# A diffusion transformer layer: half of the conditioning sum computed on ScalarE and GpSimd instead of VectorE

## The chip, the cores and the metric

The kernel runs on one core of one Trainium2 chip. The metric is the device time of one execution in microseconds (us), as the median of several runs. TensorE does the matmuls (PE in the profile, PEld its weight loads), VectorE is DVE, ScalarE is ACT, GpSimd is POOL, and SyncE (SP) issues nearly all transfers.

## The reference, cut to what matters

One layer with 1024 latent tokens and 256 context tokens, 1024 features, all in fp32. It is half a SwiGLU feed-forward, then token mixing (a 2-D Fourier transform beside a bidirectional chunkwise mLSTM), then the second half of the feed-forward. Each part is normalised and modulated by a shift, a scale and a gate that come from a conditioning vector:

```python
def ada_params(cvec, w, b):
    m = jax.nn.silu(cvec) @ w + b
    return m.reshape(cvec.shape[0], N_ADA, 1, D_MODEL)

def half_ffn(h, shift, scale, gate, g_pre, g_post, w13, w2):
    u = modulate(rmsnorm(h, g_pre), shift, scale)
    return h + 0.5 * gate * rmsnorm(swiglu(u, w13, w2), g_post)
...
    ml = ada_params(c, w_ada[l], b_ada[l])
    mc = ada_params(c_ctx[None], w_ada[l], b_ada[l])
    h_lat = half_ffn(h_lat, ml[:, 0], ml[:, 1], ml[:, 2], g[0], g[1], w13_a[l], w2_a[l])
    h_ctx = half_ffn(h_ctx, mc[:, 0], mc[:, 1], mc[:, 2], g[0], g[1], w13_a[l], w2_a[l])
```

There are two conditioning vectors, one for the latent tokens and one for the context, and both meet the same matrix `w_ada` (1024 x 9216), which is read in nine chunks of 1024 columns. Of these the context stream needs the first five.

## The kernel before

**The products.** Feed-forward products on the latent tokens use Winograd's scheme for 2 x 2 blocks: seven products in place of eight. Every fp32 operand is split in two parts, `hi` (cast on ScalarE, L145) and `lo` (the rest, subtracted on VectorE, L146), and `mm3` (L153) makes three matmuls of them. So each operand tile costs one ScalarE cast and one VectorE subtraction before TensorE can use it.

**The stage around the change.** `wino_out` is the second product of the feed-forward half. Its seven products (in the order 1, 6, 7, 4, 5, 3, 2) each run over 11 blocks of features and 4 column blocks of 128. For each block it loads weights (`raw` into `wr`, L733, or `held` into `g`, L738), combines them on VectorE (L727), splits them into `wh` and `wl`, loads the activations (`t<-gx`, L774) and splits these into `g` tiles. "The first second product" is the call in the first half of the layer.

**The background work.** Beside the matmuls, `tick` (called once per three matmuls) takes steps of generators that `later` has put in a list. During the first second product these are: the context tokens being loaded and transposed (`load_x`), the conditioning sums of chunks 2 and 3 (`ada_rest`, L239), the normalised context (`prenorm`), the conditioning sums of chunk 4, and, as results come, the residual sums.

**The conditioning sum.** For each half chunk (512 columns) `ada_rest` loads eight tiles of `w_ada` of 128 x 512 (L247) and sums them, weighted per partition by the conditioning vector, into one accumulator for each stream: a plain scaling for the first tile (L251) and `acc = t * sc + acc` for the other seven (L253), on VectorE. The two accumulators are then split, summed over the partitions by four matmuls with a selecting matrix (L263), copied (L266), turned into a column (L275) and given their bias (L279). Stream 0 is the latent, stream 1 the context. Tiles come from the pool `u` (16 buffers of 128 x 512) in chunks 2 and 3; in chunk 4 the weight tiles come from `wa` (two buffers).

**What sets the order.** The kernel is written for a scheduler that takes each instruction's place in the program as its priority, puts the instructions of each engine in a fixed order, gives tiles their buffers and adds the semaphores. Every engine then runs its own list strictly in order, and so does SP's queue of transfers. A change of who computes what can therefore move other instructions too.

Of the kernel before, what the change touches and what calls it, by code (L numbers as in the profile page):

```python
# [12 lines left out]
AF = mybir.ActivationFunctionType  # L13
ALU = mybir.AluOpType
# [5 lines left out]
CTX = 256  # L20
# [14 lines left out]
class Kernel:  # L35
# [200 lines left out]
            nc.scalar.copy(row[:2, :], pt[:2, :])  # L236
            self.ada_cols(row, (0, 1), ch, 0)

    def ada_rest(self, streams, chunks, tags=("wa", "u", "u", "b"), halves=(0, 1)):  # L239
        nc = self.nc  # L240
        w = self.a["w_ada"][0]
        for ch in chunks:
            for hf in halves:
                acc = {s: self.s512(tags[1]) for s in streams}
                for k in range(ND):
                    t = self.s512(tags[0])
                    nc.sync.dma_start(t, w[k * P : (k + 1) * P, ch * D + hf * TB : ch * D + (hf + 1) * TB])  # L247
                    yield
                    for s in streams:
                        if k == 0:  # L250
                            nc.vector.tensor_scalar_mul(acc[s], t, self.sc[:, k, s : s + 1])  # L251
                        else:
                            nc.vector.scalar_tensor_tensor(acc[s], t, self.sc[:, k, s : s + 1], acc[s],  # L253
                                                           op0=ALU.mult, op1=ALU.add)
                yield
                for s in streams:
                    ah, al = self.s512(tags[2], F32R), self.s512(tags[2], F32R)
                    self.split_act(ah, al, acc[s])
                    if s == streams[0]:
                        pr = self.aux()  # L260
                    yield
                    for i, part in enumerate((ah, al)):
                        nc.tensor.matmul(pr[:2, :], self.sel[:, s, :], part, start=s == streams[0] and i == 0,  # L263
                                         stop=s == streams[-1] and i == 1)
                row = self.s512(tags[3])
                nc.scalar.copy(row[:2, :], pr[:2, :])  # L266
                yield
                self.ada_cols(row, streams, ch, hf)
# [1333 lines left out]
    def run(self):  # L1602
        nc, a = self.nc, self.a
# [6 lines left out]
        xl, xc = [[], []], []  # L1610
# [3 lines left out]
        u = self.new_u()  # L1614
# [17 lines left out]
        for p in range(3):  # L1632
# [5 lines left out]
        gx = self.scratch([7, FF // 2, TB], "gx")  # L1638
        rc1, r1 = [], [[], []]
        self.ffn_in(w13, 11, u, U, gx, 6, mid)  # L1640
        self.later(self.load_x(a["ctx"][0], CTX, "c", xc, tag="u"), self.ada_rest([0, 1], [2, 3], "uuuu"),
                   rate=3.5)
        self.credit = -9.0
        uc = ctx_u([self.slot("u", F32R) for _ in range(ND)])

        def ctx_in():
            yield from self.prenorm(self.reload(xc[0], CTX), xc[1:], CTX, 1, 0, uc)
            yield from self.ada_rest([0, 1], [4])
        self.later(ctx_in(), rate=3.5)
        res = [[None] * ND for _ in range(NB)]  # L1650

# [32 lines left out]
        for b in range(NB):  # L1684
# [3 lines left out]
            t = self.s512("o")  # L1688
# [16 lines left out]
        for h in range(HEADS):  # L1705
# [11 lines left out]
            k = [self.qk_proj(8 + 2 * h + i, u2) for i in range(2)]  # L1717
# [19 lines left out]
        for b in range(NB):  # L1737
# [8 lines left out]
            if b == 0:  # L1746
                u = self.new_u()
# [62 lines left out]
```

## Time and profile before

| | |
|---|---|
| median of 3 runs | 2758.67 us (2755.25 to 2763.62) |
| the profiled execution's own time | 2761.97 us |
| its span in the profile | 2760.1 us |
| busy: PE, DVE, ACT, POOL | 2661.3, 1857.2, 1106.8, 100.6 us |
| the first second product | from 490.0 us to 744.1 us |

The span is what the profiler saw between the first and the last instruction; what lies around it is 1.9 us. TensorE's busy time hides small gaps, because matmuls overlap and their ends are modelled, so the number of matmuls in a stretch says more than its busy time. In a row of groups the columns are: line, engine, operation, output and inputs, shapes, count, then total busy time and mean duration in ns, and the engine's idle time before those instructions with what ended it. In a row of the timeline the first number is the start and the second the length of a run of equal instructions.

### The profile page before, as it was taken

The page shows a single profiled execution, that of the slowest core. Times are in us where ns is not written, and L with a number is a line of the kernel's source. Part 1 is how long each engine was busy: PE and PEld are TensorE (multiplying, and loading weights), DVE is VectorE, ACT ScalarE, POOL GpSimd, SP SyncE. Part 2 cuts the span into 40 slices and gives each one's busy share as a digit, 9 for nine tenths or more (in the row PEclk, how much of TensorE's full clock was granted, in tenths as well). Part 3 has the DMA queues.
Part 4 walks back from the last instruction along what each step waited for, and adds up shares of the span by engine and source line. Part 5 has one row for each costly group of instructions (what it writes and reads, how often), then busy time and mean ns, then how long its engine had stood idle before and what let it go on. Part 6 is the DMA issues. An engine that isn't in the chain of part 4 may idle for free.

```text
span 2760.1 us, 33923 instructions
## 1 busy us (share of the span) xinstructions
PE 2661.3 (96%) x11657; PEld 2114.7 (77%) x11657; DVE 1857.2 (67%) x3341; ACT 1106.8 (40%) x1893; POOL 100.6 (4%) x217
## 2 busy tenths in 40 slices
PE   8899999998999999999999999999999999998998
PEld 5688888776877777777777778778887788887776
DVE  5688887899786438565363674555667887863765
ACT  4543332444454337233333333433345433333552
POOL 1100000000000001000000000000001000000000
PEclk9999999999999999999999999999999999999999
DMA  9765454857686545325223452356556654536874
GB/s 300 242 206 164 155 167 133 309 190 252 210 252 211 170 134 173 102 69 155 79 77 103 133 142 77 94 150 196 181 157 210 183 169 153 168 107 198 293 247 139
DMA packets 426012, 472.51 MB, mean 171 GB/s; under 512 B 25497, under 2 KB 264642, under 8 KB 425840
## 3 DMA queue, kind: packets, MB, share of 16 engines
q1 hardware_dynamic: 424448, 468.53, 54.2%
q0 software_dynamic: 1248, 1.75, 0.2%
q8 instruction: 92, 1.51, 0.2%
q14 instruction: 80, 0.66, 0.1%
q10 hardware_dynamic: 144, 0.07, 0.0%
HBM read 373.21 MB, written 97.04 MB: 170 GB/s over the span
## 4 chain that ended last, share of the span: by engine, by line
PE 75%; DVE 9%; DMA 8%; issue 4%; ACT 2%; SPq 1%; POOL 0%; DVEq 0%; POOLq 0%; ACTq 0%
PE mm L153 67%; DMA m<-r_l 2%; PE aux L1147 2%; PE qc L1332 1%; DVE u L253 1%; DVE wl L141 1%; DVE g L146 1%; DMA ld<-in_w_ada_dram 1%; DMA ld<-h 1%; DMA u<-h 1%; DMA ld<-hn 1%; PE mm L234 1%; DMA t<-gx 0%; ACT wh L140 0%; DVE wl L146 0%
## 5 line engine op out<-in xcount | busy, mean ns | idle before, releaser
L153 PE MATMUL mm<-g,wh 128*128 128x512 f32 (+1 forms) x2552 | 839.6, 409 | 11.9 <-ACT g L145 5.0
L153 PEld LDWEIGHTS mm<-g,wh 128*128 128x128 f32 (+1 forms) x2552 | 484.2, 192 | 122.2 <-ACT wh L145 6.0
L153 PE MATMUL mm<-g,wl 128*128 128x512 f32 (+1 forms) x1276 | 510.7, 402 | 3.4 <-DVE wl L146 3.3
L153 PE MATMUL mm<-g,o 128*128 128x512 f32 x2112 | 497.7, 394 | 0.0
L153 PEld LDWEIGHTS mm<-g,o 128*128 128x128 f32 x2112 | 396.9, 188 | 93.7
L141 DVE TENSOR_TENSOR wl<-wr,wh 128x1024 fp32r<-128x1024 f32 x226 | 278.8, 1234 | 223.9 <-ACT wh L140 223.2
L140 ACT CAST wh<-wr 128x1024 fp32r<-128x1024 f32 x226 | 236.3, 1046 | 352.5 <-PE mm L153 307.3
L153 PE MATMUL mm<-wh,g 128*128 128x512 f32 x1032 | 331.2, 399 | 6.6 <-ACT g L145 3.9
L153 PEld LDWEIGHTS mm<-g,wl 128*128 128x128 f32 (+1 forms) x1276 | 243.8, 191 | 59.0 <-DVE wl L146 5.6
L153 PE MATMUL mm<-u,wh 128*128 128x512 f32 (+1 forms) x848 | 268.4, 398 | 7.5 <-DVE m L704 4.9
L153 PEld LDWEIGHTS mm<-wh,g 128*128 128x128 f32 x1032 | 194.1, 188 | 54.5 <-ACT g L145 4.1
L153 PE MATMUL mm<-wl,g 128*128 128x512 f32 x516 | 205.1, 397 | 0.0
L153 PEld LDWEIGHTS mm<-u,wh 128*128 128x128 f32 (+1 forms) x848 | 159.8, 190 | 46.0 <-DVE m L704 5.4
L153 PE MATMUL mm<-wh,u 128*128 128x512 f32 x544 | 176.4, 399 | 0.0
L153 PE MATMUL mm<-u,wl 128*128 128x512 f32 (+1 forms) x424 | 167.3, 397 | 2.3 <-DVE wl L141 2.3
L582 DVE TENSOR_TENSOR t<-mm,t 128x512 f32<-128x512 f32 x128 | 88.1, 688 | 78.8 <-PE mm L153 78.6
L146 DVE TENSOR_TENSOR g<-t,g 128x512 fp32r<-128x512 f32 x154 | 103.0, 687 | 38.9 <-ACT g L145 32.1
L153 PEld LDWEIGHTS mm<-wh,u 128*128 128x128 f32 x544 | 102.0, 188 | 22.5
L145 ACT CAST o<-wa 128x512 fp32r<-128x512 f32 x88 | 54.6, 622 | 156.0 <-PE mm L153 144.8
L145 ACT CAST wh<-wr 128x1024 fp32r<-128x1024 f32 (+1 forms) x72 | 62.5, 870 | 131.9 <-PE mm L153 55.2
L153 PEld LDWEIGHTS mm<-wl,g 128*128 128x128 f32 x516 | 97.2, 188 | 23.0 <-issue 0.7
L153 PE MATMUL mm<-wl,u 128*128 128x512 f32 x272 | 108.8, 400 | 2.1 <-DVE wl L141 2.1
(469 smaller groups left out, 3432.8 us busy)
## 6 DMA issues: line engine op xcount, KB each, us to landing
wr<-in_w_a_dram SPq DMA_DIRECT2D x124, 512.0 KB, 4.4
t<-gx SPq DMA_DIRECT2D x174, 256.0 KB, 4.0
wr<-in_w_in_dram SPq DMA_DIRECT2D x80, 512.0 KB, 3.8
wr<-in_w_b_dram SPq DMA_DIRECT2D x70, 512.0 KB, 4.5
gx<-m SPq DMA_DIRECT2D x88, 256.0 KB, 4.2
gx<-t SPq DMA_DIRECT2D x66, 256.0 KB, 4.3
ld<-in_w_ada_dram SPq DMA_DIRECT2D x64, 256.0 KB, 2.8
ld<-h SPq DMA_DIRECT2D x48, 256.0 KB, 3.8
```

Source lines behind the costliest of these rows:

```text
L140: nc.scalar.copy(hv, rv)
L141: nc.vector.tensor_tensor(lv, rv, hv.bitcast(F32), op=ALU.subtract)
L145: self.nc.scalar.copy(hi, src)
L146: self.nc.vector.tensor_tensor(lo, src, hi.bitcast(F32), op=ALU.subtract)
L153: mul = lambda x, y, start, stop: self.nc.tensor.matmul(out, x, y, start=start, stop=stop, skip_group_check=grown)
L234: nc.tensor.matmul(pt[:2, :], self.sc[:, k, :], t, start=k == 0, stop=k == ND - 1)
L253: nc.vector.scalar_tensor_tensor(acc[s], t, self.sc[:, k, s : s + 1], acc[s], op0=ALU.mult, op1=ALU.add)
L582: add = lambda o, x, y: nc.vector.tensor_tensor(o, x, y, op=ALU.add)
L1147: nc.tensor.matmul(pt[:, :257], kw[:, i * P : (i + 1) * P], vaug, start=True, stop=True)
L1332: nc.tensor.matmul(pt[:, :257], at(q, i, c), C[:, i * 257 : (i + 1) * 257], start=i == 0, stop=i == 1)
```

## The change

`ada_rest` gets a switch `shared`, on in the two calls beside the first second product (chunks 2, 3 and 4, thus six halves). With it, the context stream's term is computed in two steps: ScalarE multiplies the tile by the conditioning vector (the first one straight into the accumulator, the others into a new tile of the pool `u`), and GpSimd adds the new tile to the accumulator. The latent stream stays on VectorE. The two other calls of `ada_rest` stay as they were.

```diff
-    def ada_rest(self, streams, chunks, tags=("wa", "u", "u", "b"), halves=(0, 1)):
+    def ada_rest(self, streams, chunks, tags=("wa", "u", "u", "b"), halves=(0, 1), shared=False):
...
                     for s in streams:
-                        if k == 0:
+                        if shared and s == 1:
+                            part = self.s512(tags[1]) if k else acc[s]
+                            nc.scalar.activation(part, t, AF.Copy, scale=self.sc[:, k, s : s + 1])
+                            if k:
+                                nc.gpsimd.tensor_tensor(acc[s], acc[s], part, op=ALU.add)
+                        elif k == 0:
                             nc.vector.tensor_scalar_mul(acc[s], t, self.sc[:, k, s : s + 1])
...
-        self.later(self.load_x(a["ctx"][0], CTX, "c", xc, tag="u"), self.ada_rest([0, 1], [2, 3], "uuuu"),
+        self.later(self.load_x(a["ctx"][0], CTX, "c", xc, tag="u"), self.ada_rest([0, 1], [2, 3], "uuuu", shared=True),
...
-            yield from self.ada_rest([0, 1], [4])
+            yield from self.ada_rest([0, 1], [4], shared=True)
```

The lines of the changed kernel stand six further down from the accumulating step on: L253 becomes L259, L727 becomes L733, L774 becomes L780; the load of the weight tile is L248 there, the new scaling on ScalarE L253 and the new addition L255.

The scheduler gives the whole stage another order. On VectorE, in a half of chunk 3 of the kernel before (`u_5154` and `u_5155` are the two accumulators, `u_5187` and so on the weight tiles):

```order
721 L146 TENSOR_TENSOR g_5273<-t_5270,g_5272 128x512
722 L727 TENSOR_TENSOR wr_5317<-wr_5317,g_4260 128x512
723 L253 SCALAR_TENSOR_TENSOR u_5154<-u_5187,sc,u_5154 128x512
724 L253 SCALAR_TENSOR_TENSOR u_5155<-u_5187,sc,u_5155 128x512
725 L253 SCALAR_TENSOR_TENSOR u_5154<-u_5197,sc,u_5154 128x512
726 L253 SCALAR_TENSOR_TENSOR u_5155<-u_5197,sc,u_5155 128x512
727 L253 SCALAR_TENSOR_TENSOR u_5154<-u_5207,sc,u_5154 128x512
728 L253 SCALAR_TENSOR_TENSOR u_5155<-u_5207,sc,u_5155 128x512
```

The same engine in a half of chunk 3 in the changed kernel (`u_4991` is the latent accumulator):

```order
694 L259 SCALAR_TENSOR_TENSOR u_4991<-u_5015,sc,u_4991 128x512
695 L146 TENSOR_TENSOR g_5520<-t_5517,g_5519 128x512
696 L146 TENSOR_TENSOR g_5526<-t_5523,g_5525 128x512
697 L146 TENSOR_TENSOR g_5582<-t_5579,g_5581 128x512
698 L146 TENSOR_TENSOR g_5588<-t_5585,g_5587 128x512
699 L259 SCALAR_TENSOR_TENSOR u_4991<-u_5048,sc,u_4991 128x512
700 L146 TENSOR_TENSOR wl_5307<-wr_5308,wh_5306 128x1024
701 L146 TENSOR_TENSOR g_5649<-t_5646,g_5648 128x512
702 L146 TENSOR_TENSOR g_5700<-t_5697,g_5699 128x512
703 L146 TENSOR_TENSOR g_5706<-t_5703,g_5705 128x512
704 L259 SCALAR_TENSOR_TENSOR u_4991<-u_5060,sc,u_4991 128x512
```

The context steps are gone, and the latent ones no longer stand next to each other: three to four instructions of the product lie between two of them.

On ScalarE in the changed kernel, at the end of that half (`u_4992` is the context accumulator, `u_5126` the last of the scaled tiles that GpSimd adds to it):

```order
439 L253 ACTIVATE u_5114<-u_5105,sc 128x512
440 L145 CAST g_5831<-t_5829 128x512
441 L145 CAST g_5837<-t_5835 128x512
442 L253 ACTIVATE u_5126<-u_5117,sc 128x512
443 L145 CAST wh_5509<-wr_5511 128x1024
444 L145 CAST u_5135<-u_4991 128x512
445 L145 CAST g_5892<-t_5890 128x512
446 L145 CAST u_5169<-u_4992 128x512
447 L145 CAST g_5898<-t_5896 128x512
```

The scalings stand between the casts of the product's operands, and the cast of the finished context accumulator stands four places behind the last scaling.

In SP's queue of transfers, the kernel before and then the changed one, in a half of chunk 3 (`u` are weight tiles of the conditioning, `t` and `wr` tiles of the product):

```order
419 L774 DMA t_5467<-gx 128x512
420 L247 DMA u_5187<-in_w_ada_dram 128x512
421 L247 DMA u_5197<-in_w_ada_dram 128x512
422 L247 DMA u_5207<-in_w_ada_dram 128x512
423 L247 DMA u_5217<-in_w_ada_dram 128x512
424 L247 DMA u_5240<-in_w_ada_dram 128x512
425 L247 DMA u_5278<-in_w_ada_dram 128x512
426 L247 DMA u_5288<-in_w_ada_dram 128x512
```

```order
415 L248 DMA u_5015<-in_w_ada_dram 128x512
416 L780 DMA t_5646<-gx 128x512
417 L780 DMA t_5697<-gx 128x512
418 L780 DMA t_5703<-gx 128x512
419 L248 DMA u_5048<-in_w_ada_dram 128x512
420 L780 DMA t_5758<-gx 128x512
421 L780 DMA t_5764<-gx 128x512
422 L780 DMA t_5829<-gx 128x512
423 L248 DMA u_5060<-in_w_ada_dram 128x512
```

Seven loads in a row became one load behind every three others. The matmuls of the product itself keep their order; the last matmuls of the conditioning sum (L263) stand behind matmul 658 of the stage's 924 before, and behind matmul 790 in the changed kernel.

## The prediction

> **What bounds the kernel now.** I read the page's head, then the stretch the change touches: the second product of the first feed-forward half, whose background loop holds the edited generator. Its first and last matmuls, two in mid-stage, and busy time in pieces (columns: length, busy time and instructions of PE, PEld, DVE, ACT, POOL, granted clock, DMA share, GB/s):
>
> ```profile
> span 2760.1 us, 33923 instructions
> 490.00 1.52 PE L153 MATMUL mm<-g,wh 128*128 128x512 f32 x2 [4.96 <-ACT g L145]
> 519.27 0.62 PE L153 MATMUL mm<-g,wh 128*128 128x512 f32 x2
> 519.95 0.62 PE L153 MATMUL mm<-g,wh 128*128 128x512 f32 x2
> 744.12 0.39 PE L153 MATMUL mm<-wh,u 128*128 128x512 f32 x1
> 490.00:540.00 50.00, 50.00 (x206) 39.88 (x207) 42.47 (x71) 24.40 (x43) 0.00 (x0) 0.94 0.86 309
> 540.00:590.00 50.00, 44.48 (x180) 33.22 (x179) 46.51 (x79) 20.90 (x39) 0.00 (x0) 0.93 0.59 200
> 590.00:640.00 50.00, 46.35 (x202) 36.15 (x202) 46.90 (x79) 24.66 (x42) 0.00 (x0) 1.00 0.74 237
> 640.00:690.00 50.00, 44.46 (x169) 32.19 (x168) 44.99 (x68) 23.60 (x36) 0.00 (x0) 0.90 0.77 247
> 690.00:744.00 54.00, 53.90 (x248) 44.41 (x247) 41.27 (x64) 23.87 (x37) 2.40 (x2) 1.00 0.69 219
> ```
>
> The stage runs from 490.0 to 744.1: 254.1 us. It holds 924 matmuls (7 products x 11 x 4 x 3). Three take 519.95 - 519.27 = 0.68, so 0.229 each and 211.6 for all; the 24 that sum the conditioning and the small transposes add some 10. So 33 us are lost, about 5 of them at the start (the matmuls stand 0.43 apart until 496, at a lower clock). The other 28 lie between 540 and 690, where DVE is busy 138 of 150 us, ACT 69 and POOL never. DVE is what PE waits for there, directly or through ACT:
>
> ```profile
> ACT wh L145 <- DVE g L727: 19.5, 9, 6.4
> ACT wh L145 <- DVE wr L727: 16.1, 4, 6.8
> ACT u L145 <- DVE u L253: 12.6, 5, 4.4
> L253 DVE SCALAR_TENSOR_TENSOR u<-u,sc,u 128x512 f32<-128x512 f32 x56 | 37.9, 745 | 0.3 <-DMA u<-in_w_ada_dram 0.3
> L253 DVE SCALAR_TENSOR_TENSOR u<-wa,sc,u 128x512 f32<-128x512 f32 x28 | 19.5, 748 | 4.1 <-DMA wa<-in_w_ada_dram 4.1
> 590.29 0.88 DVE L251 TENSOR_SCALAR u<-u,sc 128x512 f32<-128x512 f32 x2 [1.01 <-DMA u<-in_w_ada_dram]
> 594.42 9.37 DVE L253 SCALAR_TENSOR_TENSOR u<-u,sc,u 128x512 f32<-128x512 f32 x14 [0.31 <-DMA u<-in_w_ada_dram]
> 603.71 1.22 DVE L146 TENSOR_TENSOR wl<-wr,wh 128x1024 fp32r<-128x1024 f32 x1
> 604.84 0.68 DVE L146 TENSOR_TENSOR u<-u,u 128x512 fp32r<-128x512 f32 x1
> 605.45 0.68 DVE L146 TENSOR_TENSOR g<-t,g 128x512 fp32r<-128x512 f32 x1
> ```
>
> 84 accumulating steps of the conditioning stand in this stage, in bursts of up to 14. DVE's instructions overlap, so I cost them by their pitch: 14 take 9.37, hence (9.37 - 0.74)/13 = 0.66 per step; 0.40 per plain scaling (0.88 - 0.48); 1.13 for 128x1024 (604.84 - 603.71); 0.60 for 128x512 (605.45 - 604.84).
>
> A check by these pitches: up to the matmul numbered 673 of the stage, DVE must have done (counted in the program's order, up to the write that matmul waits for) 148 of 0.60, 84 of 0.66, 12 of 0.40, 16 of 1.13, 16 half-size ones of 0.40 and small ones for 1: 175.4 us. PE's 672 matmuls take 153.9. DVE is 21.5 behind at its worst point, which is most of the 28.
>
> **The change, part by part.** *Removed from DVE:* 42 steps and 6 scalings: 42 x 0.66 + 6 x 0.40 = 30.1 us. The bursts go too: in the new order one step stands every four or five DVE instructions. The same count for the new order is worst at two places. Before matmul 577 DVE has 147 of 0.60, 28 of 0.66, 4 of 0.40, 13 of 1.13: 124.2 against PE's 131.9, 7.7 ahead. Before matmul 721 it has 166, 35, 5, 20 and 16 half-size: 155.1 against 164.9, 9.8 ahead. If nothing else happened, DVE would no longer hold PE up.
>
> *Added on GpSimd:* 42 additions of 128x512 from SBUF. The trace has 16 such, and DVE beside them:
>
> ```profile
> L455 POOL TENSOR_TENSOR b<-u,u 128x512 f32<-128x512 f32 x8 | 17.5, 2192 | 150.0 <-ACT b L367 79.4 <-DVE g L146 47.4 <-DVE acc L341 23.2
> L456 POOL TENSOR_TENSOR wa<-u,u 128x512 f32<-128x512 f32 x8 | 12.0, 1502 | 35.2 <-DVE u L409 13.0 <-ACT m L678 11.2 <-DVE g L146 6.6
> 128.73 1.65 POOL L456 TENSOR_TENSOR wa<-u,u 128x512 f32<-128x512 f32 x1 [1.23 <-DVE m L475]
> 131.00 1.70 POOL L455 TENSOR_TENSOR b<-u,u 128x512 f32<-128x512 f32 x1 [0.63 <-DVE g L146]
> 135.74 1.28 POOL L456 TENSOR_TENSOR wa<-u,u 128x512 f32<-128x512 f32 x1 [3.03 <-DVE g L146]
> 129.17 1.75 DVE L146 TENSOR_TENSOR g<-b,g 128x512 fp32r<-128x512 f32 x1
> 130.85 0.74 DVE L458 SCALAR_TENSOR_TENSOR ld<-ld,pre,rb 128x512 f32<-128x512 f32 x1
> 131.51 1.75 DVE L146 TENSOR_TENSOR g<-b,g 128x512 fp32r<-128x512 f32 x1
> 2133.50 2.97 POOL L455 TENSOR_TENSOR b<-u,u 128x512 f32<-128x512 f32 x1 [7.89 <-DVE g L146]
> 2135.22 0.68 DVE L704 TENSOR_TENSOR m<-mm,t 128x512 f32<-128x512 f32 x1
> 2135.82 1.20 DVE L146 TENSOR_TENSOR g<-wa,g 128x512 fp32r<-128x512 f32 x1
> ```
>
> A DVE instruction with two inputs in SBUF, 0.68 alone, takes 1.75 when it starts under a GpSimd addition: 1.07 more, until the addition is nearly over. The one that reads PSUM (mm) at 2135.22 keeps its 0.68, and the next loses only 0.52. Where DVE was idle nothing is lost. Over the 16 additions DVE's instructions are longer by 9.1 us, 0.57 each, with 0 and 1.07 as the ends. In this stage DVE reads PSUM in only some two dozen instructions, but without the 30 us it has more gaps. I take s = 0.75 per addition, between the mean and the end, for the stage is denser than the mean.
>
> The Trainium skill's page "SBUF — State Buffer", section "Who interferes with whom", says that DVE and GpSimd share a port pair, that a DVE instruction with two SBUF inputs contends with a GpSimd instruction that reads SBUF, and that the later one waits for the whole of the earlier. Taken to the letter an addition costs its own length, 1.28, and the change loses; the rows bear out the wait, but for 1.07 at most and less beside PSUM reads.
>
> With s, DVE's lag is 28s - 7.7 at matmul 577 and 35s - 9.8 at 721: for s = 0.57, 8.3 and 10.2; for 0.75, 13.3 and 16.5; for 1.05, 21.7 and 27.0. Against 21.5 before, s = 0.75 gains 5.0. The trace lost 28 where this count gives 21.5 (each wait is followed by matmuls at a lower clock, 0.90 to 0.93 above), so I scale by 1.3: **-6.5 us**, between -17 (s = 0.5, lag 7.7) and +7 (s = 1.05).
>
> *Added on ACT:* 48 scalings.
>
> ```profile
> 745.46 1.15 ACT L340 ACTIVATE b<-o 128x512 f32<-128x512 f32 x2
> L145 ACT CAST u<-u 128x512 fp32r<-128x512 f32 x12 | 7.3, 620 | 12.7 <-DVE u L253 12.6
> u<-in_w_ada_dram SPq DMA_DIRECT2D x32, 256.0 KB, 5.3
> ```
>
> Two take 1.15, so 0.52 each, 25 us in all. ACT is busy 117 of the stage's 254 us, so its length is hidden; without that cover it would cost the 25. What counts is order: the cast of the finished sum (u<-u) stands in ACT's queue, with the casts of PE's operands behind it, and now waits for the last addition on GpSimd instead of DVE's last step. The old wait was 12.6 over five casts. The last addition follows the last scaling by its own 1.3 to 1.7, and a late chain adds one more addition: some 2 to 3 us in each of six halves. Bounds -5 to +10; I take **+2**.
>
> *Moved: the weight loads.* SP's queue issued seven of a half's eight loads in a row; now one stands behind every two to four others, and both DVE and ACT use it six or so DVE instructions after the release that lets SP reach it. Six instructions are 4 us plus one s, the landing 5.3 (median). So up to 1 us of wait per load, on two in-order engines, where a half used to pay it once. Part falls into time in which GpSimd adds anyway. 32 loads: 0 to +15; I take **+2**. The 14 loads into two wa buffers waited before (4.1 above) and still do.
>
> *Behind the stage:* eight fewer DVE instructions of other work are done at its last matmul, so 8 x 0.60 = 5 us of DVE work pass into the next stage: 0 to +3, taken **+1**.
>
> Sum: -6.5 + 2 + 2 + 1 = -1.5. The profiled execution took 2761.97 (1.9 around its span); 3.3 above the median of the runs shown, 2758.67. From the median: **2757**.
>
> **Rivals.** *A, the additions fall into DVE's gaps.* After the change DVE has 222 - 30 = 192 busy of 254; the 62 us left exceed 42 x 1.07 = 45. For: an addition gets in most easily when DVE pauses, and the even order pauses more often. Against: the gaps stand where DVE waits for ACT, and DVE's next instruction is then what PE wants. s = 0.5 gives -17 and, with the other terms at +2, 2758.67 - 15 = 2744.
>
> *B, the port decides: slower.* DVE, being late, runs without gaps, and each addition takes its 1.05: +7; and additions wait as the one at 2133.50 did (2.97), so the chain of seven ends late and ACT stands at the cast: +6 more, loads +2: 2774. It decides from s = 0.95 on, where 35s - 9.8 passes the 21.5 of before and the three other terms are still to pay. For it: DVE's busy 92% between 540 and 690. The skill's rule, at 1.28 throughout, would give 35 x 1.28 - 9.8 = 35, hence +18 and about 2780.
>
> *C, the loads decide.* Each of the 32 loads stops DVE and ACT by 0.6 us: +19, less what the additions overlap, some 7: 2770. Against: DVE waited for these loads only 0.3 and 4.1.
>
> That the change leaves the order as it was is ruled out by the program's order.
>
> **How the numbers follow.** Changes within 0.3% (8.3 us) are what a measurement of this kernel can't tell from none. Forecast 0.40 (all of it same), A 0.28 (faster), B 0.20 and C 0.12 (slower): faster 0.28, same 0.40, slower 0.32. The forecast's own range is 2750 to 2766; reaching into both sides until two in ten are left out gives 2743 to 2774.
>
> **What would show it.** In the changed profile: DVE's busy time in the stage must fall by much less than 30 us, with 128x512 instructions of 1.2 to 1.75 among those of 0.68; their excess over 42 additions is s. If it is near 0.5 and the stage ends before 730, A holds. If additions average over 2 us and ACT's wait for POOL exceeds 12.6, B. If DVE's waits for u<-in_w_ada_dram exceed 15, C. The forecast is wrong in its base if the stage shortens by 20 us though s is 0.75: then the bursts, and not DVE's total, held PE up.

## The result, and the profile after

The changed kernel takes 2775.57 us (median of 6 runs, 2768.50 to 2780.88) beside 2758.43 us for the kernel before (median of 6): a ratio of 1.0057, with a 95% interval of 1.0040 to 1.0075. That is 16 us slower, between 11 and 21 (the two medians by themselves lie 17 apart). The forecast was 2757, its range 2743 to 2774. A second comparison, with 6 and 29 runs, gave 1.0058 (1.0041 to 1.0076). The prediction was wrong.

From here on VectorE, ScalarE, GpSimd and TensorE stand as DVE, ACT, POOL and PE, as in the profile. The page's head and busy line for the changed kernel:

```profile
span 2779.0 us, 34068 instructions
PE 2665.8 (96%) x11657; PEld 2123.6 (76%) x11657; DVE 1867.0 (67%) x3293; ACT 1137.1 (41%) x1941; POOL 174.3 (6%) x259
```

48 instructions were taken off DVE, and its busy time rose by 9.8 us (1857.2 before). Here is the stage in stretches, first of the kernel before as a whole, then of the changed kernel as a whole and in pieces (columns: length, busy time and instructions of PE, PEld, DVE, ACT, POOL, granted clock, DMA share, GB/s):

```profile
490.00:744.10 254.10, 239.28 (x1000) 185.92 (x1001) 222.24 (x357) 117.53 (x196) 2.40 (x2) 0.95 0.73 242
```

```profile
490.00:754.60 264.60, 240.97 (x1000) 187.93 (x1000) 229.94 (x307) 147.12 (x243) 74.38 (x43) 0.94 0.69 230
490.00:540.00 50.00, 46.81 (x181) 36.67 (x182) 42.23 (x57) 26.65 (x47) 11.54 (x7) 0.91 0.85 296
...
640.00:690.00 50.00, 45.46 (x193) 35.34 (x192) 45.42 (x60) 29.32 (x48) 14.77 (x10) 0.97 0.74 242
690.00:740.00 50.00, 45.11 (x195) 34.48 (x194) 37.03 (x53) 23.68 (x36) 13.87 (x10) 0.93 0.43 135
```

The stage ends at 754.6 instead of 744.1: 264.6 us, 10.5 longer. DVE is busy 229.9 us of it instead of 222.2, with 50 instructions fewer. In the first piece PE issues 181 matmuls where the kernel before had 206, and in the last 195 in 50 us where it had 248 in 54; in between the changed kernel catches up (its matmul numbered 673 starts at 682.5, that of the kernel before at 682.8). The next product, from there to the first `mm<-wh,g` matmul, takes 161.1 us instead of 158.2: 2.9 more. That makes 13.4 of the 18.9 by which the two profiled spans differ. The other 5.5 are spread over the remaining 1860 us, where every engine runs the same instructions in the same order; runs of one kernel differ by as much.

The groups that answer to those shown of before, over the stage of the changed kernel (its line numbers):

```profile
L255 POOL TENSOR_TENSOR u<-u,u 128x512 f32<-128x512 f32 x42 | 73.4, 1747 | 454.8 <-issue 323.1 <-ACT u L253 117.5 <-DVE u L259 13.5
L146 DVE TENSOR_TENSOR g<-t,g 128x512 fp32r<-128x512 f32 x77 | 62.5, 827 | 5.8 <-ACT g L145 5.8
...
L259 DVE SCALAR_TENSOR_TENSOR u<-u,sc,u 128x512 f32<-128x512 f32 x28 | 29.1, 1040 | 2.3 <-DMA u<-in_w_ada_dram 2.3
...
L146 DVE TENSOR_TENSOR wl<-g,wh 128x512 fp32r<-128x512 f32 x31 | 26.1, 861 | 6.2 <-ACT wh L145 6.0
...
L253 ACT ACTIVATE u<-u,sc 128x512 f32<-128x512 f32 x32 | 23.1, 724 | 26.0 <-DMA u<-in_w_ada_dram 25.9
...
L259 DVE SCALAR_TENSOR_TENSOR u<-wa,sc,u 128x512 f32<-128x512 f32 x14 | 15.9, 1133 | 3.4 <-DMA wa<-in_w_ada_dram 3.3
...
L253 ACT ACTIVATE u<-wa,sc 128x512 f32<-128x512 f32 x16 | 11.3, 721 | 11.1 <-DMA wa<-in_w_ada_dram 11.1
```

The accumulating step on DVE took 745 ns on average before and takes 1040 and 1133 now. The 77 subtractions `g<-t,g`, which the change does not touch, went from 51.7 us to 62.5; their group before was:

```profile
L146 DVE TENSOR_TENSOR g<-t,g 128x512 fp32r<-128x512 f32 x77 | 51.7, 685 | 5.4 <-ACT g L145 5.4
```

Counted instruction by instruction over the whole stage (against the length of its kind alone, if the difference is over 0.1 us), 39 DVE instructions are lengthened, by 37.3 us together: 0.89 per addition. The change removed 30.1 us from DVE and put 37.3 back.

The timeline shows it happening (start, length), first on POOL, then on DVE in the same microseconds:

```profile
549.52 5.96 POOL L255 TENSOR_TENSOR u<-u,u 128x512 f32<-128x512 f32 x2 [13.20 <-ACT u L253]
```

```profile
551.31 0.69 DVE L146 TENSOR_TENSOR wl<-g,wh 128x512 fp32r<-128x512 f32 x1
551.91 0.69 DVE L733 TENSOR_TENSOR g<-g,g 128x512 f32<-128x512 f32 x1
552.51 1.80 DVE L259 SCALAR_TENSOR_TENSOR u<-u,sc,u 128x512 f32<-128x512 f32 x1
554.24 1.79 DVE L146 TENSOR_TENSOR g<-t,g 128x512 fp32r<-128x512 f32 x1
555.95 0.68 DVE L146 TENSOR_TENSOR wl<-g,wh 128x512 fp32r<-128x512 f32 x1
```

Two additions run in those 5.96 us, and two DVE instructions take 1.8 us where the others take 0.68 (alone, the first takes 0.75 and the second 0.69). What PE waits for in the stage (total, times, longest), in the changed kernel:

```profile
PE aux L269 <- ACT u L145: 13.9, 5, 6.5
PE mm L153 <- ACT g L145: 5.0, 1, 5.0
PE mm L153 <- ACT m L787: 3.4, 1, 3.4
```

L269 are the matmuls that sum the conditioning, and `u` is the ACT cast of the finished sum. That cast costs PE 13.9 us now; before, when the same matmuls stood in L263, it cost 1.5:

```profile
PE aux L263 <- ACT u L145: 1.5, 1, 1.5
```

While the cast is late, the product's matmuls stand behind L269 in PE's list. ACT itself waits for it on DVE:

```profile
ACT u L253 <- DMA u<-in_w_ada_dram: 25.9, 17, 3.3
...
ACT u L253 <- DMA wa<-in_w_ada_dram: 11.1, 8, 2.6
ACT u L145 <- DVE u L259: 9.3, 6, 3.0
```

None of ACT's waits in the stage is put down to POOL. But ACT does stand 37 us for weight tiles in front of its scalings, with casts behind it.

### The profile page after: what moved, and what is told of

It is laid out like the page before. It is cut to its first block, busy times and chain, and to the rows that moved or that the text cites. A ratio compares the mean times of both kernels' runs of the same rounds, so it can differ in the third digit from the quotient of the medians.

```text
span 2779.0 us, 34068 instructions
## 1 busy us (share of the span) xinstructions
PE 2665.8 (96%) x11657; PEld 2123.6 (76%) x11657; DVE 1867.0 (67%) x3293; ACT 1137.1 (41%) x1941; POOL 174.3 (6%) x259
## 3 DMA queue, kind: packets, MB, share of 16 engines
q0 software_dynamic: 1248, 1.75, 0.2%
## 4 chain that ended last, share of the span: by engine, by line
PE 53%; DMA 7%; DVE 6%; issue 4%; ACT 2%; SPq 0%; POOL 0%; DVEq 0%; POOLq 0%; ACTq 0%
PE mm L153 47%; DMA m<-r_l 2%; PE aux L1153 2%; PE qc L1338 1%; DMA u<-h 1%; DVE wl L141 1%; DMA ld<-h 1%; DMA ld<-in_w_ada_dram 1%; ACT wh L140 0%; DMA wr<-in_w_a_dram 0%; DVE acc L259 0%; PE aux L1329 0%; PE aux L1296 0%; POOL rs_r L317 0%; PE mm L1473 0%
## 5 line engine op out<-in xcount | busy, mean ns | idle before, releaser
L153 PEld LDWEIGHTS mm<-g,wl 128*128 128x128 f32 (+1 forms) x1276 | 244.5, 192 | 53.9 <-issue 0.8
L146 DVE TENSOR_TENSOR g<-t,g 128x512 fp32r<-128x512 f32 x154 | 113.9, 758 | 38.5 <-ACT g L145 31.5
L145 ACT CAST g<-t 128x512 fp32r<-128x512 f32 x154 | 91.2, 618 | 41.9 <-PE mm L153 24.7
```

The source lines that it names most:

```text
L145: self.nc.scalar.copy(hi, src)
L146: self.nc.vector.tensor_tensor(lo, src, hi.bitcast(F32), op=ALU.subtract)
L153: mul = lambda x, y, start, stop: self.nc.tensor.matmul(out, x, y, start=start, stop=stop, skip_group_check=grown)
```

## The experiments

The theory after reading the two traces, called PORT in the expectations: the additions on GpSimd lengthen VectorE's instructions by more than was taken off, and VectorE sets the stage. The rivals: LOADS (ScalarE stands for weight tiles, and casts behind it are late) and CHAIN (the cast of the sum waits for the last addition). Intervals below are the 95% intervals of the ratio, turned into us with the time of the kernel before in the same comparison.

### The additions cut to 16 and to 256 columns

```diff
-                                nc.gpsimd.tensor_tensor(acc[s], acc[s], part, op=ALU.add)
+                                nc.gpsimd.tensor_tensor(acc[s][:, :16], acc[s][:, :16], part[:, :16], op=ALU.add)
```

> The changed kernel, with each of the 42 additions on GpSimd cut to 16 of its 512 columns (so the context stream's conditioning is not summed; every instruction of every engine stands in the same order as in the changed kernel). Theory PORT: in the changed kernel VectorE's instructions were longer by 36.6 us in the stage (0.87 per addition), more than the 30.1 us taken off it, and that made the loss. Then without the long additions the excess falls below 6 us, the stage of 263 us shortens to 222 to 235, and the time is 2733 to 2745. Theory LOADS: ScalarE stands 37 us at the scalings for weight tiles, the casts of PE's operands behind it, and that made the loss. Then the stage keeps its 250 to 263 us and the time is 2764 to 2776. Theory CHAIN (the cast of the sum waits for the last addition): the same short time as PORT, but ScalarE's waits for GpSimd, which the changed kernel's trace hardly shows, would have to fall by more than 10 us.

Measured: 2748.51 us, ratio 0.9948 (0.9929 to 0.9966), so -14.4 us (-19.6 to -9.4). Its stage as a whole, with the columns as above:

```profile
489.60:726.50 236.90, 229.57 (x1000) 181.46 (x1001) 194.32 (x307) 147.15 (x243) 29.12 (x43) 0.98 0.78 258
```

The groups of its subtractions and of the narrow additions:

```profile
L146 DVE TENSOR_TENSOR g<-t,g 128x512 fp32r<-128x512 f32 x77 | 51.8, 688 | 6.6 <-ACT g L145 6.6
...
L255 POOL TENSOR_TENSOR u<-u,u 128x16 f32<-128x16 f32 x42 | 28.1, 669 | 470.4 <-issue 321.8 <-ACT u L253 127.0 <-PE mm L153 12.7
```

PE's wait for the cast of the sum:

```profile
PE aux L269 <- ACT u L145: 1.6, 2, 1.4
```

The program is the changed kernel's, instruction by instruction and in the same order on every engine; only the width of 42 instructions on POOL differs. DVE's subtractions are back at 688 ns, no DVE instruction is lengthened by 0.1 us, the stage lasts 236.9 us instead of 264.6, and PE's wait for the sum's cast falls from 13.9 to 1.6 us. The two ratios are 30 us apart. So the width of the additions costs 30 us and turns a gain of 14 into a loss of 16. CHAIN is out: none of ACT's waits in the two stages is put down to POOL. LOADS can't be the main cause: ACT still waits 26.6 us for weight tiles here (17.8 and 8.8). But the time stayed above PORT's 2733 to 2745 and the stage above its 222 to 235. The kernel before ran at 2762.20 in this comparison, 4 us above its first median, so against it the gain of 14 is at the low end of the 13 to 25 that PORT meant: 42 steps and 6 scalings less on DVE, 30.1 us by their pitch, are worth 14.

With 256 columns (`[:, :256]` in the same place; half of the context stream's sum is left out):

> The changed kernel with each addition on GpSimd cut to 256 of its 512 columns (half of the context sum is left out; same order on every engine). 512 columns cost VectorE 0.89 us per addition and 16 columns nothing. If the cost goes with the columns: about 0.45 each, 19 us, and the time half-way between the two, the kernel before + 1 us (-3 to +5). If each addition stops a VectorE instruction for a fixed time as soon as it is long enough: 0.8 to 0.9 each and the kernel before + 12 us or more.

Measured: 2757.23 us, ratio 0.9985 (0.9974 to 0.9997), so -4.1 us (-7.2 to -0.8). One addition and the DVE instructions beside it in the timeline, POOL first:

```profile
559.71 1.16 POOL L255 TENSOR_TENSOR u<-u,u 128x256 f32<-128x256 f32 x1 [4.25 <-ACT u L253]
```

```profile
559.59 0.68 DVE L146 TENSOR_TENSOR wl<-g,wh 128x512 fp32r<-128x512 f32 x1
560.19 1.24 DVE L146 TENSOR_TENSOR g<-t,g 128x512 fp32r<-128x512 f32 x1
561.35 0.68 DVE L146 TENSOR_TENSOR wl<-g,wh 128x512 fp32r<-128x512 f32 x1
```

The lengthened instruction takes 1.24 us, 0.55 more, where 512 columns made the two above 1.06 and 1.11 longer. 34 instructions are lengthened, by 17.0 us in all: 0.40 per addition, a little under the 0.45 expected, and the time is a little under the expected -3 to +5. The cost goes with the columns: 0, 17.0 and 37.3 us of lengthening gave -14.4, -4.1 and +16. The kernel breaks even at some 21 us (on the line between the last two), thus at 0.5 per addition.

### The additions on VectorE

```diff
-                                nc.gpsimd.tensor_tensor(acc[s], acc[s], part, op=ALU.add)
+                                nc.vector.tensor_tensor(acc[s], acc[s], part, op=ALU.add)
```

> The changed kernel with the 42 additions on VectorE instead of GpSimd; the scalings stay on ScalarE. PORT: VectorE pays 42 x 0.60 = 25.2 us instead of 36.6 us of lengthening, 11.4 less; times 1.3 that is 15 us, so 2760 (2753 to 2766), no faster than the kernel before by more than 5. LOADS: the scalings and their waits for the weights are as before, so 2770 to 2778.

Measured: 2755.92 us, ratio 0.9982 (0.9971 to 0.9994), so -5.0 us (-8.0 to -1.7), as PORT expected.

Its stage, the group of the additions, and ACT's waits for weights:

```profile
490.00:738.30 248.30, 232.62 (x1000) 182.96 (x1001) 219.17 (x351) 148.53 (x245) 2.01 (x2) 0.97 0.76 247
```

```profile
L255 DVE TENSOR_TENSOR u<-u,u 128x512 f32<-128x512 f32 x42 | 28.9, 688 | 0.4 <-ACT u L253 0.3
```

```profile
ACT u L253 <- DMA u<-in_w_ada_dram: 27.8, 19, 3.9
...
ACT u L253 <- DMA wa<-in_w_ada_dram: 12.6, 10, 2.5
```

The same 42 additions as DVE's own work cost it 25 us (42 x 0.60), less than the 37.3 that they cost it from GpSimd. ACT's waits for weights (27.8 and 12.6) are as long as in the changed kernel, and do no harm here.

### Extra additions beside the kernel before

```diff
                             nc.vector.scalar_tensor_tensor(acc[s], t, self.sc[:, k, s : s + 1], acc[s],
                                                            op0=ALU.mult, op1=ALU.add)
+                            if shared and s == 1:
+                                nc.gpsimd.tensor_tensor(extra, t, t, op=ALU.add)
```

> The kernel before, with all conditioning on VectorE, and beside each of the 42 later steps of the context stream one more 128x512 addition on GpSimd of the weight tile to itself, whose result nobody reads. PORT: VectorE's instructions become 0.5 to 0.9 us longer per addition, 21 to 38 us, and with the 1.3 of lost clock the time is 2785 to 2807. LOADS: additions that nobody waits for cost nothing, 2755 to 2765.

Measured: 2797.64 us, ratio 1.0130 (1.0117 to 1.0143), so +35.9 us (+32.3 to +39.5).

Its stage, and the groups of the accumulating steps and of the extra additions:

```profile
489.30:775.40 286.10, 246.34 (x1000) 188.81 (x1000) 253.53 (x356) 116.85 (x196) 62.84 (x44) 0.92 0.65 214
```

```profile
L254 DVE SCALAR_TENSOR_TENSOR u<-u,sc,u 128x512 f32<-128x512 f32 x56 | 54.6, 1036 | 0.9 <-DMA u<-in_w_ada_dram 0.9
...
L257 POOL TENSOR_TENSOR u<-u 128x512 f32<-128x512 f32 x28 | 39.2, 1399 | 399.9 <-DMA u<-in_w_ada_dram 380.3 <-DVE wr L730 18.1
```

Nobody reads these sums and nobody waits for them, but DVE's busy time rises from 222.2 to 253.5 us in the stage, which lasts 32.0 longer. 40 DVE instructions are lengthened, by 32.0 us in all, and no wait of another engine for GpSimd is on the list. This is the disputed cost nearly by itself: 42 additions that GpSimd makes for nothing cost the kernel 36 us, more than the 30.1 us of DVE work that the change moved away. Nearly, because the scheduler also changed the order of the stage's other instructions in places, so the 36 us are not the additions' alone to the last microsecond; the runs with 16, 256 and 512 columns don't have this weakness.

### Weight tiles requested one step earlier

```diff
+                wts = []
                 for k in range(ND):
-                    t = self.s512(tags[0])
-                    nc.sync.dma_start(t, w[k * P : (k + 1) * P, ch * D + hf * TB : ch * D + (hf + 1) * TB])
+                    for kk in range(len(wts), min(ND, k + 1 + shared)):
+                        t = self.s512(tags[0])
+                        nc.sync.dma_start(t, w[kk * P : (kk + 1) * P, ch * D + hf * TB : ch * D + (hf + 1) * TB])
+                        wts.append(t)
+                    t = wts[k]
                     yield
```

> The changed kernel, with each weight tile of the moved conditioning requested one step earlier (two tiles under way at once). PORT: VectorE's excess stays at 33 to 40 us and the time within 5 us of the changed kernel's 2775.6. LOADS: ScalarE's 37 us of waits for weights fall below 15, the casts behind it come earlier, and the time falls by 8 or more, to 2767 or less.

Measured: 2781.26 us, ratio 1.0072 (1.0056 to 1.0089), so +19.9 us (+15.5 to +24.6). ACT's waits for weight tiles in this kernel's stage, and PE's for the cast of the sum:

```profile
ACT u L257 <- DMA wa<-in_w_ada_dram: 12.8, 9, 3.8
...
ACT u L257 <- DMA u<-in_w_ada_dram: 6.5, 6, 3.2
```

```profile
PE aux L273 <- ACT u L145: 19.0, 6, 5.5
```

ACT waits 19.3 us for weight tiles instead of 37.0, and PE still waits for the sum's cast, 19.0 us. DVE's excess is 40.5 us. LOADS has lost: half of the waits are gone and the time did not fall. PORT's own bounds were just missed too (an excess of 33 to 40 us, a time within 5 us of 2775.6). Here ACT does wait once for the last addition before the cast of a sum, for 3.2 us, as CHAIN has it.

The same with the additions on VectorE:

> add_on_vector with each weight tile requested one step earlier. If ScalarE's waits for weight tiles (40 us in add_on_vector) still cost something once the additions no longer hold VectorE: they fall below 22 us, and the time to the kernel before - 9 or less. If they are hidden: within 3 us of add_on_vector, the kernel before - 3 to - 8.

Measured: 2759.60 us, ratio 1.0003 (0.9991 to 1.0015), so +0.8 us (-2.5 to +4.1). Its stage is 247.9 us, that of `add_on_vector` 248.3, and both leave the next product at the same point (896.0 and 895.8). ACT's waits for weight tiles fell to 24.4 us (11.1 and 13.3). So in the stage the earlier requests bring nothing. The time fits neither expectation. Against the kernel before it came out 6 us worse than `add_on_vector` (4 us in the medians), but the two intervals overlap; the traces don't show a cause.

### The change for some of the chunks alone

```diff
-            yield from self.ada_rest([0, 1], [4], shared=True)
+            yield from self.ada_rest([0, 1], [4])
```

> The change for chunks 2 and 3 alone (28 of the 42 additions); chunk 4 stays wholly on VectorE. Theory EVEN (each addition costs alike, by what it adds to VectorE less what it takes off): two thirds of the change's loss of 17 us, so the kernel before + 11 us (+7 to +15). Theory TAIL (in the changed kernel's trace the 672nd matmul of the stage stands as early as before, and the 9 us are lost after it, where chunk 4 is summed): the kernel before + 0 (-4 to +4).

Measured: 2769.53 us, ratio 1.0040 (1.0027 to 1.0053), so +11.0 us (+7.5 to +14.6). All 28 additions lengthened a DVE instruction, by 29.0 us in all; 20.1 (28 x 0.66 + 4 x 0.40) had been removed. The reverse, `shared` in chunk 4 alone:

> The change for chunk 4 alone (14 of the 42 additions); chunks 2 and 3 stay wholly on VectorE. EVEN: one third of the loss, the kernel before + 6 us (+2 to +9). TAIL: nearly all of it, the kernel before + 10 to + 17 us.

Measured: 2759.98 us, ratio 1.0005 (0.9994 to 1.0015), so +1.4 us (-1.7 to +4.1). 12 of 14 additions lengthened an instruction, by 11.3 us, against 10.0 removed. TAIL is out, although the late part of the stage is where the changed kernel's trace loses its 10 us: the additions in chunks 2 and 3 do the harm. EVEN fits the first run and is a little high for the second, where two additions cost nothing. In both, the time follows what DVE gained or lost on balance: +8.9 gave +11, +1.3 gave +1.

### Less work for VectorE without GpSimd

Both streams scaled on ScalarE, all additions on VectorE (`if shared:` in place of `if shared and s == 1:`):

> Both streams are scaled on ScalarE (96 scalings) and all 84 additions are made on VectorE; GpSimd has none. If VectorE's total sets the stage: 84 x 0.06 + 12 x 0.40 = 9.8 us less than the kernel before on VectorE, twice the 4.9 of add_on_vector, so the kernel before - 10 us (-14 to -7). If ScalarE's queue sets it (25 us more scalings than in add_on_vector, each waiting for its weight tile in front of the casts of PE's operands): no gain over add_on_vector, the kernel before - 5 to + 3 us.

Measured: 2762.95 us, ratio 1.0012 (1.0002 to 1.0023), so +3.3 us (+0.6 to +6.3). Its stage, and PE's waits in the product behind it:

```profile
489.50:735.20 245.70, 232.12 (x993) 182.38 (x993) 206.76 (x330) 172.60 (x285) 1.93 (x1) 0.97 0.73 238
```

```profile
PE mm L153 <- DVE wl L141: 4.6, 6, 1.9
PE mm L153 <- DVE o L1660: 1.6, 2, 1.4
```

The stage does shorten, by 8.4 us. In the product behind it, the kernel before lost 1.0 us to `wl` and nothing to `o`. DVE work (the residual sums) that was done by the stage's end before now stands there, and that product takes 167.9 us instead of 158.2. So neither expectation had the reason: the stage became 8.4 shorter, and the product behind it 9.7 longer. The 8.4 are no clean measure of the 9.8 taken off either: apart from the 12 scalings, 15 fewer DVE instructions stand in the stage (330 where 345 were to be expected), some 9 us of work that had only moved behind it.

Only the first scaling of each sum on ScalarE, all steps on VectorE:

```diff
-                        if shared and s == 1:
-                            part = self.s512(tags[1]) if k else acc[s]
-                            nc.scalar.activation(part, t, AF.Copy, scale=self.sc[:, k, s : s + 1])
-                            if k:
-                                nc.gpsimd.tensor_tensor(acc[s], acc[s], part, op=ALU.add)
+                        if shared and k == 0:
+                            nc.scalar.activation(acc[s], t, AF.Copy, scale=self.sc[:, k, s : s + 1])
                         elif k == 0:
```

> The kernel before with only the 12 first scalings of the six sums (both streams) on ScalarE; all 84 further steps stay on VectorE, GpSimd has none. If VectorE's net time decides: 12 x 0.40 = 4.8 us less, the kernel before - 5 us (-8 to -2). If the gain in the stage is given back behind it, as in both_scaled: 0 (-2 to +3).

Measured: 2754.67 us, ratio 0.9979 (0.9967 to 0.9992), so -5.8 us (-9.1 to -2.2), as 4.8 us less on VectorE would give. With `add_on_vector` this is the version that beats both kernels, each by less than the 0.3% that counts as a change here. `add_on_vector` for chunks 2 and 3 alone:

> add_on_vector for chunks 2 and 3 alone; chunk 4 stays as in the kernel before. If VectorE's net time decides: 28 x 0.06 + 4 x 0.40 = 3.3 us less, the kernel before - 3 us (-6 to 0), less gain than add_on_vector's 5. If ScalarE's scalings of chunk 4, with their 12 us of waits for the wa tiles, cost something in add_on_vector: the kernel before - 5 or better.

Measured: 2759.18 us, ratio 0.9993 (0.9979 to 1.0008), so -1.9 us (-5.8 to +2.2): what 3.3 us less on VectorE would give.

### The changed kernel again

> The changed kernel once more, beside the three below. The kernel before + 16 us (+11 to +20) again, VectorE's excess in the stage 35 to 40 us again; if the 17 us of the first comparison were partly chance, + 10 or less.

Measured: 2776.40 us, ratio 1.0058 (1.0041 to 1.0076), so +16.0 us (+11.3 to +21.0); the excess in its stage is 36.5 us. The loss is not chance.

## Why the prediction was wrong

All runs in one table, by DVE's work in the stage; the two last rows are `add_on_vector` with the loads one step earlier and for chunks 2 and 3 alone. "Removed" is by the pitches of the prediction, "lengthened" counted in each trace as above; busy and length come from one window over the stage, and idle is their difference. All in us.

| kernel | removed from DVE | DVE lengthened | stage | DVE busy | DVE idle | time against before |
|---|---|---|---|---|---|---|
| before | 0 | 0 | 254.1 | 222.2 | 31.9 | 0 |
| changed | 30.1 | 37.3 | 264.6 | 229.9 | 34.7 | +15.7 |
| changed again | 30.1 | 36.5 | 266.4 | 228.8 | 37.6 | +16.0 |
| 256 columns | 30.1 | 17.0 | 244.5 | 210.7 | 33.8 | -4.1 |
| 16 columns | 30.1 | 0 | 236.9 | 194.3 | 42.6 | -14.4 |
| additions on VectorE | 4.9 | 0 | 248.3 | 219.2 | 29.1 | -5.0 |
| extra additions | 0 | 32.0 | 286.1 | 253.5 | 32.6 | +35.9 |
| loads one ahead | 30.1 | 40.5 | 274.0 | 233.5 | 40.5 | +19.9 |
| chunks 2, 3 alone | 20.1 | 29.0 | 256.3 | 228.6 | 27.7 | +11.0 |
| chunk 4 alone | 10.0 | 11.3 | 249.7 | 222.4 | 27.3 | +1.4 |
| both scaled | 9.8 | 0 | 245.7 | 206.8 | 38.9 | +3.3 |
| first on ScalarE | 4.8 | 0 | 251.7 | 218.1 | 33.6 | -5.8 |
| on VectorE, loads ahead | 4.9 | 0 | 247.9 | 217.9 | 30.0 | +0.8 |
| on VectorE, chunks 2, 3 | 3.3 | 0 | 249.6 | 220.5 | 29.1 | -1.9 |

**What bounds the kernel** was right: VectorE. But the reading was not sharp enough. In every one of these traces the stage lasts as long as VectorE is busy plus 27 to 43 us, and in the kernel before and the changed one 31.9 and 34.7. The idle part does not shrink when the order is made even.

**Removed from DVE** (30.1 us) was right as a size: with the effect of the additions gone, DVE is busy 27.9 us less (222.2 to 194.3). What the prediction made of it failed. This is the first wrong step: the lag counted at the worst matmul, "7.7 ahead" and "9.8 ahead" in the new order, as if VectorE could use all of its time. With no lengthening that step promised 28 us (21.5 x 1.3), and 23 after the terms for the cast, the loads and the work behind. The 16-column run, which has no lengthening, gained 14.4. There DVE stood idle for 42.6 us of the stage instead of 31.9, and its waits for loads grew by about as much: 11.5 us for weight tiles at L259 and 4.6 for `wr` at L733, where the kernel before had 4.4 at its accumulating steps and none for `wr`. No run tests what these waits cost, so why the new order brings no more than 14 stays open.

In the other direction the step let 9.8 us of lengthening pass for free, so that 35 additions of 0.75 cost only 16.5 x 1.3 = 21.5. The runs show that lengthening counts nearly in full: 30 us of time for 37.3 us, and 36 for 32.0. These two shortfalls of about 9 us each are the miss of 17. The prediction's formula balances at s = 0.89, where 35s - 9.8 reaches 21.5 (0.95, which rival B names for this, is a slip), so even with the measured s it would have said 2764. The totals alone, 42 x s against 30.1, would have put the balance point at s = 0.72; the runs have it at about 0.5, since in the new order the stage keeps more idle time than before (34.7, 33.8 and 42.6 us with 512, 256 and 16 columns, against 31.9) and 1 to 3 us go into the product behind it. (With the pitches as printed, the prediction's three sums of DVE's work come to 174.5, 123.0 and 153.7, about 1 less than it has; that moves the forecast by less than 1 us.)

**The lengthening per addition** was the second wrong size: s = 0.75 taken, 0.89 and 0.87 measured, inside the bounds of 0 and 1.05. By the prediction's own formula the difference is 35 x 0.14 x 1.3 = 6 us, most of the second shortfall. "Denser than the mean" was right and went further: 39 of 42 additions hit an instruction. One that hits costs 1.06 (the median of the 39), as the rows of before showed.

The Trainium skill's page "SBUF — State Buffer", section "Who interferes with whom", says that of two such instructions the later one waits for the whole of the earlier. By its letter the prediction worked out 2780. The traces agree that the DVE instruction waits, and that it waits by the width of the addition (0.55 at 560.19 of the 256-column run, 1.06 for 512 columns), but the price of a hit is 1.06 and not the 1.28 of an addition alone. The prediction had the rule and gave its result no chance of its own beside rival B.

**ACT, +2 for the cast behind the additions:** no such wait arose in the changed kernel, where none of ACT's waits is put down to POOL in either run (it did in two others: 3.2 us with the loads one step earlier, 3.4 with chunk 4 alone). The cast was late because VectorE's own last step was (9.3 us of ACT's waits), and that is where PE lost most: 13.9 us at L269, 7.1 with 256 columns, 1.6 with 16.

**The loads, +2:** the place was wrong. The waits came on ACT (37 us), hardly on DVE (2.3 for `u`, 3.3 for `wa`), and in the changed kernel they seem to cost little: halving them left it as slow as it was. More of it is visible when the additions are out of the way: in the 16-column run DVE has the waits given above, and PE waits 2.7 us once for an eviction that ACT makes late, behind a scaling that waits for its weights.

**Work behind the stage, +1 (0 to +3):** 2.9 in the changed kernel, 2.0 in its second run. Near the upper end, but right. `both_scaled` shows that the term can be 10.

**The rivals.** B named the time (2774) and half of the mechanism: nearly every addition at full price, though VectorE was not without gaps (34.7 us idle). Its other half, late additions that hold ACT, did not happen: they average 1.75 us, below the 2 that the prediction set as the mark. And it was said to decide only from s = 0.95, with +7 for additions at 1.05 each. With one half of its sum absent and s at 0.89, that it came within 2 us of the time is luck. A fell with s = 0.89. C fell with the loads.

**What would show it:** the test for s was the right one and gave the answer at once. "DVE's busy time must fall by much less than 30" was itself too hopeful: it rose by 7.7.

## What to carry to other kernels

Before work goes from VectorE to GpSimd, add up the whole: what leaves VectorE, against the number of GpSimd instructions times what one costs a VectorE instruction beside it. In this kernel a two-input step of 0.66 us became an addition that took 0.89 back, so that even making it on VectorE itself was better. And when the busy engine's idle time has not gone away under earlier tuning, don't credit a better order with it: take the change of its busy time as the change of the stage (here a loss came in full or more, and of a gain of 30 us only half), and look one stage further for what was pushed there.

## What the runs showed of the hardware

- What a GpSimd addition of two SBUF operands costs a VectorE instruction that also reads two goes with its width: 1.06 us for 512 columns (median of 39 lengthened instructions, at most 1.12), 0.53 for 256 (median of 34), and no more than some 0.02 for 16, although the 16-column addition itself is recorded at 0.67 us on average. An extra addition, whose two operands are one and the same tile of 512 columns, cost 0.78 (median of 40).
- It is a wait of that length and not a slower pace: beside an addition of 512 columns, in the run with chunk 4 alone, a VectorE instruction of 128x8 took 1.27 us (at 626.55), where it takes 0.16 in the kernel before.
- It works the other way too. The two additions recorded as 5.96 us at 549.52 start while VectorE runs two-input instructions back to back, each at its normal 0.69. Only at 552.51 is the first VectorE instruction lengthened, and while it lasts the first addition ends (at 553.8). What an addition's recorded length (1.28 to 4.25 us) has above the shortest is thus waiting, and no measure of what it costs VectorE. A 16-column addition is recorded as 3.38 us (at 541.00 of the 16-column run; the shortest as 0.22), while VectorE's instructions beside it keep their 0.70.
- 42 additions whose results are never used cost a kernel some 36 us. An idle GpSimd is not free capacity beside a VectorE that is busy with two-input instructions.
